# Average pooling, 2x2x2: three 16-row, 512 B stores on ScalarE's queue in place of one 2 KB-a-row store

One core of one Trainium2 chip. The metric is device time in microseconds of the whole program, lower is better; the kernel before takes 91.7 us.

## The reference

`x` is (8, 32, 32, 32, 32) float32, 33.55 MB; the kernel size is 2. Each output element is the mean of a 2x2x2 window, so the output is (8, 32, 16, 16, 16), 4.19 MB.

```python
for i in range(out_d):
    for j in range(out_h):
        for k in range(out_w):
            window = x[:, :, 2*i:2*i+2, 2*j:2*j+2, 2*k:2*k+2]
            result[:, :, i, j, k] = np.mean(window, axis=(-3, -2, -1))
```

## The kernel before

The 256 (batch, channel) rows are two halves `t` of 128 partitions. Each half is read in four units of 32 KB a row; the last two units are each read as two half loads of 16 KB. Five input buffers are in turn. VectorE pools each unit into `obuf[t]` (16 KB a row) with three instructions. All loads go through SyncE's queue. One store of 2 KB a row goes through ScalarE's queue as soon as the fifth unit is pooled; the others follow the loads on SyncE's queue.

```python
plan = [
    (0, 0, (32,)), (0, 32, (32,)), (0, 64, (32,)), (0, 96, (32,)),
    (1, 0, (32,)), (1, 32, (32,)), (1, 64, (16, 16)), (1, 96, (16, 16)),
]
# pool_unit: tensor_add over d, tensor_add over w, tensor_tensor_reduce over h with scale 0.125
for t, k0, parts in plan:
    tin = pool_in.tile([P, 32 * KF], F32, tag="tin", name="tin")
    # one nc.sync.dma_start for each part, then pool_unit for each part   (cut)
for queue, t, k0, kb in [
    (nc.scalar, 1, 0, 2),
    (nc.sync, 0, 0, 16),
    (nc.sync, 1, 2, 12),
    (nc.sync, 1, 14, 2),
]:
    queue.dma_start(
        out=ov[t * P:(t + 1) * P, k0 * KF:(k0 + kb) * KF],
        in_=obuf[t][:, k0 * KF:(k0 + kb) * KF],
    )
```

`KF` is 256 elements, 1 KB. A scheduler places every issue where its data is ready; each store waits for its units.

Of the kernel before, what the change touches and what calls it, by code (L numbers as in the profile page):

```python
# [1 line left out]

# [4 lines left out]

F32 = mybir.dt.float32
KF = 256


@with_exitstack
def pool_rows(
    ctx: ExitStack,
    tc: tile.TileContext,
    x: bass.AP,
    kernel_size: int,
    out: bass.AP,
):
    nc = tc.nc  # L20
    assert kernel_size == 2, "only kernel_size == 2 supported"

    B, C, D, H, W = x.shape
    P = nc.NUM_PARTITIONS
    assert (B * C, D, H, W) == (2 * P, 32, 32, 32)
    add = mybir.AluOpType.add



    xv = x.rearrange("b c d h w -> (b c) (d h w)")  # L30
    ov = out.rearrange("b c d h w -> (b c) (d h w)")




    pool_in = ctx.enter_context(tc.tile_pool(name="pin", bufs=5))
    pool_out = ctx.enter_context(tc.tile_pool(name="pout", bufs=1))
    obuf = [pool_out.tile([P, 16 * KF], F32, name=f"obuf{t}") for t in range(2)]
    dummy = pool_out.tile([P, 1], F32, name="dummy")


    plan = [
        (0, 0, (32,)),
        (0, 32, (32,)),
        (0, 64, (32,)),
        (0, 96, (32,)),
        (1, 0, (32,)),
        (1, 32, (32,)),
        (1, 64, (16, 16)),
        (1, 96, (16, 16)),  # L50
    ]

    def pool_unit(buf, t, k0, kb):

        od = kb // 8
        a = buf.rearrange("p (o dd e) -> p o dd e", o=od, dd=2)
        b = buf[:, :od * 1024]
        nc.vector.tensor_add(  # L58
            out=b.rearrange("p (o e) -> p o e", o=od), in0=a[:, :, 0], in1=a[:, :, 1])
        bv = b.rearrange("p (e ww) -> p e ww", ww=2)  # L60
        c = buf[:, od * 1024:od * 1536]
        nc.vector.tensor_add(out=c, in0=bv[:, :, 0], in1=bv[:, :, 1])  # L62
        cv = c.rearrange("p (j hh k) -> p j hh k", hh=2, k=16)
        o0 = k0 * KF // 8
        nc.vector.tensor_tensor_reduce(  # L65
            out=obuf[t][:, o0:o0 + od * 256].rearrange("p (j k) -> p j k", k=16),
            in0=cv[:, :, 0], in1=cv[:, :, 1],
            scale=0.125, scalar=0.0, op0=add, op1=add, accum_out=dummy[:, :],
        )

    for t, k0, parts in plan:
        tin = pool_in.tile([P, 32 * KF], F32, tag="tin", name="tin")
        views = []
        o = 0
        for kb in parts:
            v = tin[:, o * KF:(o + kb) * KF]
            nc.sync.dma_start(  # L77
                out=v, in_=xv[t * P:(t + 1) * P, (k0 + o) * KF:(k0 + o + kb) * KF])
            views.append((v, k0 + o, kb))
            o += kb  # L80
        for v, k, kb in views:
            pool_unit(v, t, k, kb)



    for queue, t, k0, kb in [
        (nc.scalar, 1, 0, 2),
        (nc.sync, 0, 0, 16),
        (nc.sync, 1, 2, 12),
        (nc.sync, 1, 14, 2),  # L90
    ]:
        queue.dma_start(
            out=ov[t * P:(t + 1) * P, k0 * KF:(k0 + kb) * KF],
            in_=obuf[t][:, k0 * KF:(k0 + kb) * KF],
        )


def kernel(tc: tile.TileContext, x: bass.AP, kernel_size: int, out: bass.AP):
    nc = tc.nc
    pool_rows(tc, x, kernel_size, out)  # L100
    tc.close()
    tc.compile()  # L102
    blocks = nc.main_func.blocks



    opening, program = blocks[0].instructions, blocks[tc.starting_block_idx].instructions
    load = next(i for i in program if isinstance(i, mybir.InstDMACopy))
    assert load.engine == nc.sync.engine
    barrier = next(  # L110
        n for n, i in enumerate(opening)
        if i.engine == load.engine and isinstance(i, mybir.InstDrain))
    program.remove(load)
    opening.insert(barrier, load)




    closing = blocks[-1].instructions
    stores = [  # L120
        i for i in program
        if isinstance(i, mybir.InstDMACopy) and "out_" in i.outs[0].memref]
    kept = [u.id for i in stores for u in i.sync_info.on_update]
    kept = [n for j, n in enumerate(kept) if n not in kept[j + 1:]]
    final = next(
        i for i in closing
        if i.engine == nc.sync.engine and isinstance(i, mybir.InstDrain))
    waits = {w.id: w for w in final.sync_info.on_wait}
    closing[closing.index(final)] = mybir.InstDrain(
        name=final.name, engine=final.engine, ins=[], outs=[], is_reset_sema=False,  # L130
        sync_info=mybir.SyncInfo(
            on_wait=[w for n, w in waits.items() if n not in kept], on_update=[]))


    reset = next(
        n for n, i in enumerate(closing)
        if isinstance(i, mybir.InstDrain) and i.is_reset_sema)
    first, stop = closing[reset].reset_range_start, closing[reset].reset_range_stop
    assert isinstance(closing[reset + 1], mybir.InstISA)
    while len(closing) > reset:  # L140
        closing.pop()
    n = first
    while n < stop:
        m = n
        while m < stop and m not in kept:
            m += 1
        if m > n:
            closing.append(mybir.InstDrain(
                name=nc.get_next_instruction_name(), engine=nc.gpsimd.engine, ins=[], outs=[],
                is_reset_sema=True, reset_range_start=n, reset_range_stop=m))  # L150
            nc.gpsimd.sem_clear(range(n, m))
        n = m + 1
    for n in kept:
        w = waits[n]
        closing.append(mybir.InstEventSemaphore(
            name=nc.get_next_instruction_name(), engine=nc.sync.engine, ins=[], outs=[],
            sync_info=mybir.SyncInfo(
                on_wait=[w],
                on_update=[mybir.SyncUpdate(
                    sync_type="semaphore", id=n, ant_name=w.ant_name,  # L160
                    update_mode="sem-sub-imm", update_value=w.wait_value)])))


# [1 line left out]
_INS = ['x', 'kernel_size']  # L165
_OUTS = [((8, 32, 16, 16, 16), 'float32')]

_NUMBERS = {'kernel_size': 2}


# [26 lines left out]
```

## Time and profile before

| | before |
|---|---|
| time, median of 6 runs | 91.68 us (91.52 to 91.82) |
| VectorE busy | 64.1 us (74%) |
| DMA, SyncE's queue / ScalarE's queue | 98.4% / 0.8% of sixteen engines |
| HBM read / written | 33.55 / 4.19 MB |

The page's DMA shares are shares of the time of all sixteen DMA engines. The span of the profile (86.6 us) ends before the last store lands, at 90.4; a landing is the time of issue plus the page's "us to landing". The lines themselves stand in the prediction.

### The profile page before, as it was taken

How to read it: one execution, taken by the hardware profiler on the slowest of the kernel's cores; microseconds unless marked ns; L12 is line 12 of the kernel's file. 1: busy time of each engine (PE TensorE's matmuls, PEld its weight loads, DVE VectorE, ACT ScalarE, POOL GpSimd, SP SyncE). 2: the span in 40 equal slices, each digit the busy share in tenths (PEclk: the TensorE clock that was granted, in tenths of full speed). 3: DMA queues.
4: the chain of work that ended last, by engine and by line, in shares of the span. 5: the costliest groups of instructions: out<-in, count | busy, mean ns of one | idle time of the engine just before them, and what ended most of it. 6: DMA issues, size and time to landing. Idle time of an engine off the chain costs nothing.

```text
span 86.6 us, 91 instructions
## 1 busy us (share of the span) xinstructions
DVE 64.1 (74%) x40; POOL 0.2 (0%) x4
## 2 busy tenths in 40 slices
DVE  0000049993999749992999749992999999999994
POOL 0000000000000000000000000000000000000000
DMA  8889998899979999799988999699999999999999
GB/s 242 379 363 469 485 485 348 379 485 485 469 333 409 485 485 424 318 469 485 485 348 379 485 485 469 288 454 416 405 407 424 407 462 394 462 394 454 394 454 398
DMA packets 1774, 36.48 MB, mean 421 GB/s; under 512 B 192, under 2 KB 192, under 8 KB 320
## 3 DMA queue, kind: packets, MB, share of 16 engines
q1 hardware_dynamic: 1630, 36.22, 98.4%
q10 hardware_dynamic: 144, 0.26, 0.8%
HBM read 33.55 MB, written 4.19 MB: 436 GB/s over the span
## 4 chain that ended last, share of the span: by engine, by line
DMA 83%; DVE 14%; SPq 1%; issue 0%; DVEq 0%
DMA tin<-in_x_dram 83%; DVE tin L58 8%; DVE tin L62 4%; DVE obuf L65 2%; SPq L77 1%; DVE dummy L65 0%; DVEq L102 0%
## 5 line engine op out<-in xcount | busy, mean ns | idle before, releaser
L58 DVE TENSOR_TENSOR tin<-tin 128x4096 f32<-128x4096 f32 (+1 forms) x10 | 35.7, 3570 | 20.7 <-DMA tin<-in_x_dram 20.6
L62 DVE TENSOR_TENSOR tin<-tin 128x2048 f32<-128x2048 f32 (+1 forms) x10 | 18.6, 1865 | 0.3
L65 DVE CUSTOM_DVE_ANT_1 obuf<-tin 128x1024 f32<-128x1024 f32 (+1 forms) x10 | 10.1, 1011 | 0.3
L65 DVE DVE_READ_ACCUMULATOR2_ANT dummy<- 128x1 f32 x10 | 0.8, 82 | 0.0
L178 POOL MEMSET const-uint8-127<- 128x1 uint8 x1 | 0.1, 102 | 0.0
L178 POOL MEMSET const-bfloat16-1.0<- 128x1 bf16 x1 | 0.1, 101 | 0.0
L178 POOL MEMSET const-float32-0.0<- 128x1 f32 x1 | 0.1, 98 | 0.2 <-issue 0.2
L178 POOL MEMSET const-float32-1.0<- 128x1 f32 x1 | 0.1, 98 | 0.0
## 6 DMA issues: line engine op xcount, KB each, us to landing
tin<-in_x_dram SPq DMA_DIRECT2D x6, 4096.0 KB, 35.0
tin<-in_x_dram SPq DMA_DIRECT2D x4, 2048.0 KB, 38.9
out_dram<-obuf SPq DMA_DIRECT2D x1, 2048.0 KB, 36.8
out_dram<-obuf SPq DMA_DIRECT2D x1, 1536.0 KB, 8.8
out_dram<-obuf ACTq DMA_DIRECT2D x1, 256.0 KB, 9.9
out_dram<-obuf SPq DMA_DIRECT2D x1, 256.0 KB, 4.9
```

The costliest lines, as they stand in the source:

```text
L58: nc.vector.tensor_add(out=b.rearrange("p (o e) -> p o e", o=od), in0=a[:, :, 0], in1=a[:, :, 1])
L62: nc.vector.tensor_add(out=c, in0=bv[:, :, 0], in1=bv[:, :, 1])
L65: nc.vector.tensor_tensor_reduce(out=obuf[t][:, o0:o0 + od * 256].rearrange("p (j k) -> p j k", k=16), in0=cv[:, :, 0], in1=cv[:, :, 1], s ...
L77: nc.sync.dma_start(out=v, in_=xv[t * P:(t + 1) * P, (k0 + o) * KF:(k0 + o + kb) * KF])
L178: nc = _bacc.Bacc("TRN2", target_bir_lowering=False, num_devices=1)
```

## The change

Its intent is to let only tiny transfers come between the loads, and to keep the 256 KB for the tail. Three stores of 16 rows x 512 B go out on ScalarE's queue after the first, third and fifth unit; the full SyncE stores write the same bytes once more later.

```diff
-    for queue, t, k0, kb in [
-        (nc.scalar, 1, 0, 2),
-        (nc.sync, 0, 0, 16),
-        (nc.sync, 1, 2, 12),
-        (nc.sync, 1, 14, 2),
-    ]:
-        queue.dma_start(
+    for t, k0 in [(0, 0), (0, 8), (1, 0)]:
+        nc.scalar.dma_start(
+            out=ov[t * P:t * P + 16, k0 * KF:k0 * KF + 128],
+            in_=obuf[t][:16, k0 * KF:k0 * KF + 128])
+    for t, k0, kb in [(0, 0, 16), (1, 0, 14), (1, 14, 2)]:
+        nc.sync.dma_start(
             out=ov[t * P:(t + 1) * P, k0 * KF:(k0 + kb) * KF],
             in_=obuf[t][:, k0 * KF:(k0 + kb) * KF],
         )
```

## The prediction

> **What bounds the kernel now.** I began with the page's summary, because it says which resource is full. VectorE is busy 74% of the span, the DMA row is at 8 or 9 tenths nearly everywhere, and the scalar queue (q10) is a very small part of the traffic:
>
> ```profile
> DVE 64.1 (74%) x40; POOL 0.2 (0%) x4
> DMA packets 1774, 36.48 MB, mean 421 GB/s; under 512 B 192, under 2 KB 192, under 8 KB 320
> q1 hardware_dynamic: 1630, 36.22, 98.4%
> q10 hardware_dynamic: 144, 0.26, 0.8%
> ```
>
> 98.4% and 0.8% make 99.2% of sixteen engines' time over the whole span. To see whether that is a plateau or an average, I took the timeline, where each 4 MB load releases one large addition on VectorE:
>
> ```profile
> 12.12 4.42 DVE L58 TENSOR_TENSOR tin<-tin 128x4096 f32<-128x4096 f32 x1 [12.12 <-DMA tin<-in_x_dram]
> 21.81 4.43 DVE L58 TENSOR_TENSOR tin<-tin 128x4096 f32<-128x4096 f32 x1 [1.68 <-DMA tin<-in_x_dram]
> 31.53 4.43 DVE L58 TENSOR_TENSOR tin<-tin 128x4096 f32<-128x4096 f32 x1 [1.70 <-DMA tin<-in_x_dram]
> ...
> 60.67 4.43 DVE L58 TENSOR_TENSOR tin<-tin 128x4096 f32<-128x4096 f32 x1 [1.69 <-DMA tin<-in_x_dram]
> ...
> 80.95 0.08 DVE L65 DVE_READ_ACCUMULATOR2_ANT dummy<- 128x1 f32 x1
> ...
> 81.18 2.29 DVE L58 TENSOR_TENSOR tin<-tin 128x2048 f32<-128x2048 f32 x1
> ```
>
> The loads land 9.71 us apart (21.81 less 12.12, and so on; five intervals take 48.55 us), and VectorE idles 1.7 us in each. One load is 4.194 MB, so the rate is 432 GB/s. The busy share by windows agrees and places the one irregular stretch:
>
> ```profile
> 31.53:41.25 9.72, 7.95 (x5) 0.00 (x0) 1.00 1.00 432
> 50.96:60.67 9.71, 7.95 (x5) 0.00 (x0) 1.00 0.98 420
> 60.67:81.18 20.51, 20.16 (x17) 0.00 (x0) 1.00 1.01 425
> 81.18:86.60 5.42, 4.21 (x4) 0.00 (x0) 1.00 0.95 406
> ```
>
> (Columns: stretch, length, VectorE busy, GpSimd busy, clock, DMA share, GB/s.) The share is 1.00 wherever there are only loads.
>
> The chain of waits ends in VectorE's last 4.3 us, which suggests a tail of "last load, pool, store". That is misleading, and the list of DMA issues shows why:
>
> ```profile
> out_dram<-obuf SPq DMA_DIRECT2D x1, 2048.0 KB, 36.8
> out_dram<-obuf SPq DMA_DIRECT2D x1, 1536.0 KB, 8.8
> out_dram<-obuf ACTq DMA_DIRECT2D x1, 256.0 KB, 9.9
> out_dram<-obuf SPq DMA_DIRECT2D x1, 256.0 KB, 4.9
> ```
>
> The timeline has SyncE issuing these three stores at 49.3, 81.1 and 85.5 us. They land at 49.3 + 36.8 = 86.1, 81.1 + 8.8 = 89.9 and 85.5 + 4.9 = 90.4. The 2 MB store sits behind the loads in SyncE's queue and lands 86.1 - 81.18 = 4.9 us after the last load, which is 2.097 MB at 432 GB/s; the 1.5 MB store takes the next 3.8 us, and the 256 KB the last 0.5. So the engines go from loads to stores without a pause, and the last store was in the queue some 4 us before they got to it. The end is set by the sum of bytes through sixteen full engines: 37.75 MB / 432 GB/s = 87.4 us. The rest of 91.57 is the start (12.12 less one period, 2.4 us), some small costs and 1.2 us after the last landing.
>
> **What the Trainium skill says.** "DMA: Bandwidth & Descriptors", section "Where 436 GB/s comes from", gives 435.2 GB/s as the ceiling of sixteen SBUF ports; the measured 432 is 99% of it, so the loads have nothing left to gain. The same page, "Issuing engines are not separate DMA queues", says that transfers issued on ScalarE and SyncE run on the same sixteen engines and interleave. The trace agrees: the ScalarE store, issued at 59.0 amid loads, took 9.9 us to land for bytes that need 0.6. Its section "Queues, rings and completion order" says each engine goes round its queues packet by packet; so a tiny store costs its own packet and cannot hold up the loads for long. "Specifications" puts the size for line rate at 512 B and above, just what each tiny row has; no run yet shows one here.
>
> **The change part by part.** All per engine, since the engines share each transfer equally; a 16-row store gives each engine one row if it is spread over all sixteen.
>
> 1. *Removed: the 256 KB store on ScalarE.* q10 took 0.8% of 86.6 us = 0.69 us of each engine. It had 144 / 16 = 9 packets per engine, and the bytes alone need 0.262 MB / 432 GB/s = 0.61 us, so a packet costs about 0.009 us beyond its bytes. Minus 0.69.
> 2. *Moved: those 256 KB into the second SyncE store*, 12 KB a row becoming 14 KB, with no packets added. Plus 0.61. Items 1 and 2 give -0.08.
> 3. *The interruption of the loads.* From 60.67 to the last load's release at 81.18 are 20.51 us. The two units of two half loads each are two periods, 19.42; the ScalarE store is 0.69; the half-size packets double the data packets from 16 to 32 per engine, 16 x 0.009 = 0.14. That leaves 0.26 us unaccounted for. It is in the stretch where the ScalarE store entered (DMA share 0.98 and 420 GB/s just before 60.67). If the store caused it, removing it is worth up to -0.26; if the smaller load packets did, 0.
> 4. *Added: three tiny stores.* 512 B at 27 GB/s per engine is 0.019 us, plus a data and a semaphore packet at 0.009 each: 0.037, three times 0.11. If an interruption costs by the event, up to 3 x 0.26 = 0.78 more; by the packet (one against eight), 3 x 0.03 = 0.10.
> 5. *Waits.* The three tiny stores take part in the rotation of completion semaphores. The instruction order of the changed kernel shows that a later half load then also waits for the first tiny store, the last half load for the fourth load, the 2 MB store for the second tiny one and the next store for the third. The last half load's issue, now at about 40, is put off to the landing at 41.25. Nothing comes of it: it lands 41 us after issue, four transfers deep. The tiny stores come from units done at about 20, 40 and 59, and are waited for at about 30, 49 and 81; even with the 9.9 us that the old store took they are in time.
> 6. *VectorE* runs the same 42 instructions; 64.1 us with slack. The last load may land 0.7 to 0.9 us earlier since the 256 KB are now behind it, but that only lengthens the last store's time in the queue.
>
> The sum with item 3 at half and item 4 by the packet: -0.08 - 0.13 + 0.11 + 0.10 = 0.00. Tiny stores among full-size loads are less likely to disturb than nine packets in a row of half loads, so I lean to a small gain: 91.5 us.
>
> **The rivals.**
> - *A shorter tail.* One could say that loads released 0.8 us earlier make the end 0.8 us earlier: 90.8. For it speaks the chain of waits, which passes through the last load and VectorE. Against it the landing times: the stores pour out at full rate until 90.4 with their issues some 4 us early, and the 256 KB that left the loads' way are in that tail.
> - *Every entry of the second queue costs by the event.* Then three cost up to 0.78 and the removal gives 0.26 back: about 92.0. For it speaks only the 0.26 of item 3, which is not shown to be the store's.
> - *A tiny store is late and holds a load or a store back.* Something must then be late by more than the queue's depth, two whole loads (about 19 us) at the half loads' issue; a stall would show as DMA below 1.00 and cost microseconds, 94 or more. Against it stand the margins of item 5, 9 us or more each.
> - *The early writes spare a later cost*, of the first write to each stretch of output. In the kernel before, the 2 MB store writes a part of the output never written before and still lands at the full-rate 4.9 us, so nothing is there to spare; it would be 91.5 again.
>
> **Range and chances.** The terms are tenths of a microsecond and their signs partly cancel; the three runs before span 0.3 us. I put 91.5, from 91.1 to 92.0. Two per cent is 1.8 us, more than twice the largest term in either direction, and I know nothing in the profile that could give it except a stall from the waits. Faster 0.02, same 0.96, slower 0.02.
>
> **What would show it right or wrong.** Right: loads still 9.71 us apart; q10 at about 0.1% instead of 0.8%; the larger store's landing about 0.6 us later after the 2 MB store's than now, and the last landing within 0.3 us of 90.4; the last load's release near 80.4. Item 3 is decided by the stretch from the sixth load's release to the last half load's: 19.6 if the store caused the excess, 19.8 if not. Wrong: a dip of the DMA share at an issue of SyncE, load periods longer than 9.8 after a tiny store, or an end that moves by more than 0.5 us with the same DMA share.

## The result, and the profile after

| | before | after |
|---|---|---|
| time, median of 6 runs | 91.68 us (91.52 to 91.82) | 92.10 us (92.05 to 92.27) |
| ratio | | 1.0051, 95% interval 1.0037 to 1.0065 |

A ratio is the mean time of one kernel's runs over that of the other's runs of the same rounds, so it is not quite the ratio of the medians. Executions over 1.5% slower than the fastest of the same kernel are left out of the means. The change costs 0.4 us: within 2%, as expected, but 0.1 us above the predicted range, and in the direction that I had not leaned to.

DMA queues and issues in the page of the changed kernel:

```profile
q1 hardware_dynamic: 1633, 36.35, 99.2%
q10 hardware_dynamic: 96, 0.02, 0.1%
...
out_dram<-obuf SPq DMA_DIRECT2D x1, 2048.0 KB, 36.5
out_dram<-obuf SPq DMA_DIRECT2D x1, 1792.0 KB, 9.0
out_dram<-obuf SPq DMA_DIRECT2D x1, 256.0 KB, 5.4
out_dram<-obuf ACTq DMA_DIRECT2D x3, 8.0 KB, 6.4
```

ScalarE's share fell to 0.1% as foreseen, and the engines are as full as they were. The SyncE stores were issued at 49.3, 81.1 and 85.3 us, so they land at 85.8, 90.1 and 90.7. Before it was 86.1, 89.9 and 90.4. The 2 MB store is 0.3 us earlier, not the 0.7 to 0.9 by which the prediction let the last load land earlier, and the larger second store then turns that into 0.3 us later.

Where the missing 0.5 us went is seen in windows of 4 us: the one in which the ScalarE store entered (60 to 64) and the one just ahead of the first big SyncE store (76 to 80). The last two columns are the DMA share and GB/s. Before:

```profile
60.00:64.00 4.00, 3.33 (x1) 0.00 (x0) 1.00 0.97 381
...
76.00:80.00 4.00, 3.93 (x5) 0.00 (x0) 1.00 1.07 451
```

After:

```profile
60.00:64.00 4.00, 3.30 (x1) 0.00 (x0) 1.00 0.99 420
64.00:76.00 12.00, 11.90 (x10) 0.00 (x0) 1.00 1.02 433
76.00:80.00 4.00, 3.93 (x5) 0.00 (x0) 1.00 0.97 356
```

A packet counts in the window in which it starts, so neither column alone is safe in a short window; GB/s over the share is. It is the rate of the sixteen engines while they are busy: 433 / 1.02 = 425 among half loads, and 381 / 0.97 = 393 and 356 / 0.97 = 367 in the two bad windows. So the engines are not idle there, but their load packets take longer. In 76 to 80 us of the changed kernel the loss is 4 x 0.97 x (1 - 367/425) = 0.53 us of every engine; in the kernel before it is nothing there (451 / 1.07 = 421) and 4 x 0.97 x (1 - 393/425) = 0.29 us at 60 to 64.

The packets in the trace say it exactly (in the kernel before and after, a packet is one row's piece of a transfer on one engine, or a semaphore's update, the signal that an engine has done its share). A 16 KB load packet takes 0.611 us nearly everywhere, but two in a row on most engines (one on the others) took 0.8 to 1.1 us; they started from 77.5 to 79 us, just before the last load's shares landed (80.15 to 80.95 us). I call the sum of such excess, over all packets and divided by sixteen engines, the *stretch*: 0.58 us in 74 to 82 us after the change, against 0.07 there and 0.34 at 58 to 74 before it. The engines also part company: the last half load's sixteen shares land within 0.80 us of each other (before 0.39), the last store's within 0.77 (before 0.42). The program ends 1.39 us after the *slowest* engine's last landing in both, so what counts is 90.37 against 90.70. The mean of the last store's sixteen landings moved less, from 90.11 to 90.25: the other 0.19 us of the 0.33 come from engines that lost unequally (in the second profiles of both kernels, shown further down, the mean moves by 0.09 of 0.13 us).

### The profile page after: what moved, and what is told of

Its sections match the earlier page's. It is cut to its first block, busy times and chain, and to the rows that moved or that the text cites. A ratio compares the mean times of both kernels' runs of the same rounds, so it can differ in the third digit from the quotient of the medians.

```text
span 86.4 us, 94 instructions
## 1 busy us (share of the span) xinstructions
DVE 64.0 (74%) x40; POOL 0.2 (0%) x4
## 4 chain that ended last, share of the span: by engine, by line
DMA 61%; DVE 37%; issue 0%; DVEq 0%
DMA tin<-in_x_dram 61%; DVE tin L58 21%; DVE tin L62 11%; DVE obuf L65 6%; DVE dummy L65 0%; DVEq L102 0%
```

## The experiments

My theory after this (A): when the loads first meet a bulk store, every engine loses some half microsecond, once. The old ScalarE store took that loss early and more cheaply; the tiny stores do not. Its rival (C): the tiny stores, their semaphores (the counters by which an engine waits for a transfer) or the later issue of the last half load are to blame. Four kernels at a time shared a chip and the runs of the kernel before. The edits below are abridged and show what differs from the changed kernel. Each kernel has one profile, of one execution.

**No tiny stores** (e1_none).

```diff
-    for t, k0 in [(0, 0), (0, 8), (1, 0)]:
-        nc.scalar.dma_start(...)
```

> The changed kernel without its three tiny stores; the 2 KB are still in the second SyncE store. Theory A (the 256 KB store on ScalarE paid early for a cost that comes when loads first meet a store over all 128 rows; the tiny stores do not pay it, so it is paid by the last half load now): 92.0 us, the tiny stores' 0.11 us gone and nothing else; DMA in 76 to 80 us as in the changed kernel (356 GB/s at a share of 0.97). Theory C (the tiny stores themselves, their semaphore order or the later issue of the last half load slow it): 91.5 us, and 450 GB/s in 76 to 80 us.

Measured: 91.97 us (91.87 to 92.15), ratio to before 1.0028 (1.0015 to 1.0041).

```profile
76.00:80.00 4.00, 3.93 (x5) 0.00 (x0) 1.00 0.97 352
```

The slow window is there with no tiny store in the program. C falls for the larger part: about 0.26 us of the slowdown is there without them. The rest is 0.08 to 0.13 us by the medians of the changed kernel (92.05 and 92.10) and 0.07 to 0.21 by the ratios, which agrees with the 0.11 of the prediction but is not measured more closely than that.

**One ScalarE store of 128 rows x 512 B** (e2_128rows_512B).

```diff
+    nc.scalar.dma_start(out=ov[P:2 * P, 0:128], in_=obuf[1][:, 0:128])   # for the tiny ones
```

> One store on ScalarE of 128 rows of 512 B from the fifth unit in place of the three tiny ones, eight packets per engine, written again by the full SyncE store. Theory A (rows or packets per engine count): the cost is paid near 60 us, 76 to 80 us goes at about 450 GB/s, and the time is 91.9 us (0.11 off, 0.23 on for the packets, 0.34 off for the cost). Theory B (it is the bytes that count, and 64 KB are too few): 76 to 80 us stays near 356 GB/s and the time is 92.2 us.

Measured: 92.13 us, ratio 1.0042 (1.0027 to 1.0057), 356 GB/s at 0.97 in 76 to 80 us. In this profile eight packets of 512 B per engine, on all rows, did not take the loss early.

**One ScalarE store of 16 rows x 16 KB** (e3_16rows_16KB).

```diff
+    nc.scalar.dma_start(out=ov[0:16, 0:4096], in_=obuf[0][:16, 0:4096])   # for the tiny ones
```

> One store on ScalarE of 16 rows of 16 KB from the first half's finished output (ready at 49 us), as many bytes as the old 2 KB store but one packet per engine; written again by SyncE, so 0.62 us of engine time more. Theory B (bytes count): 76 to 80 us at about 450 GB/s, 92.3 us. Theory A (rows or packets count): 76 to 80 us at about 356 GB/s, 92.6 us.

Measured: 92.61 us (92.26 to 92.68, five runs), ratio 1.0084 (1.0066 to 1.0102); a sixth run, at 93.83, is not used.

```profile
48.00:52.00 4.00, 2.21 (x3) 0.00 (x0) 1.00 1.09 410
...
76.00:80.00 4.00, 3.93 (x5) 0.00 (x0) 1.00 0.97 418
```

In this profile a single 16 KB packet per engine goes with a loss at another place: the rate while busy is 376 GB/s at 48 to 52 us, and 431 where the changed kernel had 367. In the trace the stretch is 0.50 us at 50 to 52 us and 0.005 in 74 to 82. So here the loss is taken once, and nothing of it returns after the 24 us of loads that follow. My reading, "by the first store that is big enough", is not shown: the next kernels speak against it. The time of 92.6 shows that taking it early earns nothing by itself: it lies 0.64 us above the kernel without tiny stores, and the extra packets are 0.62. One thing more differs: SyncE's 2 MB store waited for this store and was issued at 57.2 us and not at 49.3, still some 24 us before the engines came to it.

**The 2 KB store, from the first unit at 20 us** (e4_early_2KB).

```diff
+    nc.scalar.dma_start(out=ov[0:P, 0:512], in_=obuf[0][:, 0:512])        # for the tiny ones
+    # SyncE: (0, 512:4096), (1, 0:3584), (1, 3584:4096)
```

> The 2 KB store on ScalarE as in the kernel before, but from the first unit at 20 us (output rows of the first half) and not from the fifth at 59 us; nothing is written twice. If an early store over all rows pays the cost for good (theory A): 91.7 us, like the kernel before, with 76 to 80 us at about 450 GB/s. If it must lie close before the big stores, or on the other half's rows: 92.0 us with 76 to 80 us near 356 GB/s.

Measured: 92.04 us, ratio 1.0027 (1.0014 to 1.0040), 365 GB/s at 0.98 in 76 to 80 us; stretch 0.09 us at 24 to 32 us and 0.52 in 74 to 82. The same number of bytes at another time, and for the other half of the rows, neither takes the loss nor helps. My theory A in its simple form, "any early bulk store over all rows", falls.

**The 2 KB store at 49 us** (g1_2KB_at49).

```diff
+    nc.scalar.dma_start(out=ov[0:P, 3584:4096], in_=obuf[0][:, 3584:4096])
+    # SyncE: (0, 0:3584), (1, 0:3584), (1, 3584:4096)
```

> The 2 KB store on ScalarE taken from the fourth unit at 49 us instead of the first at 20; nothing written twice. If an early bulk store helps only when it comes close before the big stores (theory T, time): it pays near 53 us or later, 76 to 80 us goes at about 450 GB/s, 91.7 us. If what counts is that it meets 16 KB load packets and not 32 KB ones (theory L): its packets mostly meet 32 KB loads (from 53 to 60 us), 76 to 80 us stays at or near 356 GB/s, 92.0 us.

Measured: 91.99 us, ratio 1.0018 (1.0001 to 1.0036), 401 GB/s at 1.02 in 76 to 80 us, stretch 0.23 us up to 58 us and 0.33 in 74 to 82. The loss is split in two here, in an execution that took 91.72 us, the fastest of the six; the median is the time that theory L gave, the window lies between.

**16 rows x 4 KB** (g2_16rows_4KB).

```diff
+    nc.scalar.dma_start(out=ov[0:16, 0:1024], in_=obuf[0][:16, 0:1024])   # for the tiny ones
```

> As the 16 rows of 16 KB, with 4 KB a row: one 4 KB packet per engine at 49 us, written again by SyncE (0.16 us of engine time). If the cost is an amount that is paid in parts (theory S): about 0.15 us of longer load packets near 50 us, 0.4 us left for 76 to 80 us (some 380 GB/s), 92.1 us. If it is paid in one go by whatever is big enough (theory E): either nothing near 50 us and 356 GB/s in 76 to 80 us, 92.1 us, or all of it near 50 us and 420 GB/s or more in 76 to 80 us, 92.1 us as well; the windows decide, not the time.

Measured: 92.06 us, ratio 1.0026 (1.0009 to 1.0042), 389 GB/s at 1.00 in 76 to 80 us. I had overlooked that 4 KB a row is all from the first unit, so this store went out at 20 us and not at 49. Its own packets left no mark (0.01 us of stretch at 22 to 24), and stretches of 0.43 us in all from 38 to 64 us had no store packet near them. They did not spare the loss of 0.39 in 74 to 82 us. It decides nothing between S and E, and it speaks against theory A: load packets are also lengthened where no store enters.

**1 KB a row at 59 us** (g3_1KB_at59).

```diff
+    nc.scalar.dma_start(out=ov[P:2 * P, 0:256], in_=obuf[1][:, 0:256])
+    # SyncE: (0, 0:4096), (1, 256:3584), (1, 3584:4096)
```

> The kernel before with 1 KB a row instead of 2 KB in the ScalarE store at 59 us, the rest in the second SyncE store; nothing written twice. Theory S: half of the 0.3 us near 60 us and 76 to 80 us between 356 and 451 GB/s, near 400; 91.85 us. Theory E: like the kernel before or like the one without tiny stores, 91.7 or 92.0 us.

Measured: 91.95 us (91.54 to 92.26), ratio 1.0009 (0.9984 to 1.0034), in its profile (at 92.15) 369 GB/s at 1.05 and a stretch of 0.77 us in 74 to 82. Executions of one kernel differ by 0.7 us here. That the loss varies as much from one to the next is likely, but not shown, as one of them was profiled. Nothing of it was taken early in this profile, against S.

**The early 2 KB store, third and fourth load split** (g4_early_2KB_halfloads).

```diff
-        (0, 64, (32,)),  (0, 96, (32,)),
+        (0, 64, (16, 16)),  (0, 96, (16, 16)),     # and the store as in e4_early_2KB
```

> The early 2 KB store from the first unit at 20 us, with the third and fourth loads split into two halves each, so that its packets meet 16 KB load packets. Splitting adds 16 packets per engine (0.14 us). Theory L (16 KB load packets): about 0.3 us of longer load packets near 24 us, 76 to 80 us at about 450 GB/s, 91.85 us. Theory T (time): 356 GB/s in 76 to 80 us, 92.2 us.

Measured: 91.82 us (91.73 to 92.22), ratio 1.0013 (0.9994 to 1.0032): the time of theory L. Its windows were not: 393 GB/s at 1.01 in 76 to 80 us, with a stretch of 0.37 in 74 to 82 and 0.10 before 58.

**The 2 KB store put back beside two tiny ones** (h1_tiny_and_2KB), the most direct test.

```diff
-    for t, k0 in [(0, 0), (0, 8), (1, 0)]:     # the third tiny store becomes
+    for t, k0 in [(0, 0), (0, 8)]:             # 128 rows x 2 KB again
+    nc.scalar.dma_start(out=ov[P:2 * P, 0:512], in_=obuf[1][:, 0:512])
+    # SyncE: (0, 0:4096), (1, 512:3584), (1, 3584:4096)
```

> The changed kernel with its third tiny store widened back to the 256 KB store (128 rows of 2 KB, which then leaves the second SyncE store); the first two tiny stores, the rotation of semaphores and the later issue of the last half load stay. Theory A (the loss is the missing 2 KB store): 91.75 us, the kernel before plus two tiny stores of 0.037; 76 to 80 us at about 450 GB/s. Theory C (the tiny stores or their waits): 92.0 us or more.

Measured: 91.85 us (91.72 to 91.86), ratio 1.0008 (0.9995 to 1.0022).

```profile
60.00:64.00 4.00, 3.29 (x1) 0.00 (x0) 1.00 1.03 430
76.00:80.00 4.00, 3.93 (x5) 0.00 (x0) 1.00 1.02 393
```

On the same chip the changed kernel took 92.05 (91.97 to 92.22) and the kernel before 91.84 and 91.74. With the same rotation of semaphores and the same late half load as the changed kernel, the time is that of the kernel before. What slows the changed kernel is the missing 2 KB store; why it does, this does not show. The window of 450 GB/s that I expected did not come: that store makes the loss smaller, and does not always take it early.

**Two 2 KB stores, at 49 and 59 us** (h2_two_2KB).

```diff
+    # ScalarE: (0, 3584:4096) and (1, 0:512), 128 rows each
+    # SyncE: (0, 0:3584), (1, 512:3584), (1, 3584:4096)
```

> Two 2 KB stores on ScalarE over all 128 rows, from the fourth unit at 49 us and from the fifth at 59, nothing written twice. If each takes a share of the switch's cost and lets the engines arrive at it closer together: 91.5 to 91.7 us, and 76 to 80 us at 450 GB/s. If an early store merely moves the cost: 91.7 to 91.8 us.

Measured: 91.79 us, ratio 1.0003 (0.9989 to 1.0018), 426 GB/s at 1.05. No gain over one, which answers the question of a better version: none was found.

**Both kernels once more** (h3_before_again, h4_after_again; no edit).

> The kernel before once more, for a second profile. If its smooth passage into the big stores is a property and not one lucky profile: 91.7 us, 76 to 80 us at 440 GB/s or more, last landings of the sixteen engines within 0.45 us of each other. If not: anything from 356 to 451 GB/s.

> The changed kernel once more, for a second profile. If the slow switch is a property: 92.1 us, 76 to 80 us at about 356 GB/s, last landings spread over 0.6 us or more. If it is chance: as the kernel before in some profiles.

Measured: before 91.84 us, ratio 1.0008 (0.9993 to 1.0023); after 92.05 us, ratio 1.0036 (1.0022 to 1.0051). The windows of the second profile of before, then of after:

```profile
60.00:64.00 4.00, 3.36 (x1) 0.00 (x0) 1.00 1.03 432
76.00:80.00 4.00, 3.93 (x5) 0.00 (x0) 1.00 1.00 393
```

```profile
60.00:64.00 4.00, 3.03 (x1) 0.00 (x0) 1.00 0.99 420
76.00:80.00 4.00, 3.93 (x5) 0.00 (x0) 1.00 1.00 381
```

The difference in time repeats. The smooth passage of the first profile of before was luck: in this one the loss sits in front of the big stores as well, only smaller (stretch 0.34 in 74 to 82 us, against 0.47 after; last landings within 0.55 and 0.59 us). One profile of each kernel had shown me a cleaner story than there is.

**Control: no ScalarE store, third and fourth load split** (i2_none_halfloads).

```diff
-        (0, 64, (32,)),  (0, 96, (32,)),
+        (0, 64, (16, 16)),  (0, 96, (16, 16)),     # and no store on ScalarE
```

> Control: no store on ScalarE at all, third and fourth loads split in halves (0.16 us of packets more than the kernel without tiny stores, 91.97). If the split loads alone gave the relief: 91.8 us. If it takes the 2 KB store meeting half loads (theory L): 92.1 us.

Measured: 91.88 us (91.74 to 91.99), ratio 1.0009 (0.9992 to 1.0025), stretch 0.35 us in 74 to 82. That is 0.08 us over the kernel before by the ratio, where the unsplit kernel without early stores was at 0.26 and has 0.16 us less of packets: splitting two loads of the middle helps without any early store. Theory L is not needed to explain the time of the split kernel with the early store (91.82), and falls.

**The 2 KB store at 49 us, fifth and sixth load split** (i1_2KB_at49_halfloads).

```diff
-        (1, 0, (32,)),  (1, 32, (32,)),
+        (1, 0, (16, 16)),  (1, 32, (16, 16)),      # and the store as in g1_2KB_at49
```

> The 2 KB store from the fourth unit at 49 us, with the fifth and sixth loads split in halves so that its packets meet 16 KB load packets. Theory L: 91.9 us (0.16 for the split, 0.3 off against the 92.1 that the unsplit one would give). Otherwise 92.1 us or more.

Measured: 91.85 us (91.55 to 92.12), ratio 1.0008 (0.9988 to 1.0028); stretch 0.49 us up to 58 us, 0.004 in 74 to 82. The time fits L, but after the control it cannot speak for it.

**The first big store begun with 2 KB a row** (i4_small_first).

```diff
+    # no store on ScalarE; SyncE: (0, 0:512), (0, 512:4096), (1, 0:3584), (1, 3584:4096)
```

> No store on ScalarE; the first big SyncE store is cut into 2 KB of each row, then 14 KB, so the switch begins with 2 KB packets (0.07 us more). If the loss comes from the large first store packet: 91.75 us and 76 to 80 us above 400 GB/s. If not: 92.05 us.

Measured: 91.93 us (91.68 to 92.36), ratio 1.0017 (0.9994 to 1.0040). Inconclusive; the profile (of a run at 91.68) has 360 GB/s at 0.92 in 76 to 80 us, a stretch of 0.31.

**The 2 KB store at 59 us, written again in the tail** (i5_2KB_twice).

```diff
+    nc.scalar.dma_start(out=ov[P:2 * P, 0:512], in_=obuf[1][:, 0:512])    # SyncE as in the changed kernel
```

> The 2 KB store on ScalarE at 59 us as before, but the second SyncE store writes those bytes again, so the tail stays as long as in the changed kernel and only the store's presence differs (0.68 us of packets). If presence counts: 92.3 us. If it is the 256 KB taken out of the tail: 92.65 us.

Measured: 92.33 us (92.29 to 92.53), ratio 1.0063 (1.0049 to 1.0078).

```profile
60.00:64.00 4.00, 3.37 (x1) 0.00 (x0) 1.00 0.97 377
76.00:80.00 4.00, 3.93 (x5) 0.00 (x0) 1.00 1.03 442
```

It is the presence of the store that counts, not the 256 KB that it takes out of the tail. The time is 0.36 us above the kernel without early stores, where its packets alone would cost 0.68. Here the loss was taken early, at 60 to 64 us (389 GB/s while busy), and none of it later (429).

**All together.** The *engine work* is the sum of every packet at its usual time (32 KB 1.213 us, 16 KB 0.611, 14 KB 0.535, 12 KB 0.460, 2 KB 0.084, 512 B 0.027, a semaphore's 0.009), divided by sixteen. The *remainder* is the median time less that: start, end and whatever the engines lost.

| kernel | median us | engine work | remainder | stretch at 3-58 / 58-74 / 74-82 us |
|---|---|---|---|---|
| before | 91.68 | 87.81 | 3.87 | 0.07 / 0.34 / 0.07 |
| before, second | 91.84 | 87.81 | 4.03 | 0.05 / 0.08 / 0.34 |
| 2 KB beside two tiny (h1) | 91.85 | 87.89 | 3.96 | 0.01 / 0.10 / 0.41 |
| two 2 KB (h2) | 91.79 | 87.89 | 3.90 | 0.13 / 0.13 / 0.22 |
| 2 KB twice (i5) | 92.33 | 88.41 | 3.92 | 0.12 / 0.42 / 0.00 |
| 2 KB at 20, split (g4) | 91.82 | 87.97 | 3.85 | 0.10 / 0.10 / 0.37 |
| 2 KB at 49, split (i1) | 91.85 | 87.97 | 3.88 | 0.49 / 0.00 / 0.00 |
| none, split (i2) | 91.88 | 87.90 | 3.98 | 0.12 / 0.09 / 0.35 |
| after | 92.10 | 87.84 | 4.26 | 0.02 / 0.07 / 0.58 |
| after, second | 92.05 | 87.84 | 4.21 | 0.03 / 0.06 / 0.47 |
| none (e1) | 91.97 | 87.73 | 4.24 | 0.06 / 0.08 / 0.62 |
| 128 rows x 512 B (e2) | 92.13 | 87.96 | 4.17 | 0.05 / 0.04 / 0.57 |
| 16 rows x 16 KB (e3) | 92.61 | 88.35 | 4.26 | 0.77 / 0.00 / 0.01 |
| 2 KB at 20 (e4) | 92.04 | 87.81 | 4.23 | 0.11 / 0.03 / 0.52 |
| 2 KB at 49 (g1) | 91.99 | 87.81 | 4.18 | 0.23 / 0.01 / 0.33 |
| 16 rows x 4 KB (g2) | 92.06 | 87.90 | 4.16 | 0.36 / 0.12 / 0.39 |
| 1 KB at 59 (g3) | 91.95 | 87.81 | 4.14 | 0.04 / 0.05 / 0.77 |
| 2 KB first in the tail (i4) | 91.93 | 87.81 | 4.12 | 0.04 / 0.09 / 0.31 |

The table is sorted by the remainder: 3.85 to 4.03 us in the upper eight rows, 4.12 to 4.26 in the lower ten. The gap of 0.09 us is less than the 0.16 between the two medians of the one kernel before, so the line between them is not sharp. A second count uses the ratios, which compare runs of the same rounds: the time over the kernel before, less the engine work over it. It is within 0.1 us of zero in the upper rows. It is 0.23 to 0.44 us, clear of zero by the 95% intervals, for the changed kernel twice, e1, e2, e3 and e4. It is 0.17 for g1, just clear, and 0.08 to 0.16 for g2, g3 and i4, which are undecided. All four kernels that have the 2 KB store at 59 us are in the upper rows.

The stretch is of one profiled run and the median of all runs, so they match only roughly; and it is a mean over engines, while the time follows the slowest. In all eighteen profiles the program ended 1.37 to 1.40 us after the slowest engine's last landing.

## Why the prediction was wrong

- **The bound and the sum of bytes: right.** The engines are full from the first load to the last store. The end after the last landing is 1.39 us, not 1.2: the prediction took the landing from the profiled run (91.76 us) and the time from a median of 91.57. The packets of items 1, 2 and 4 come to 87.84 - 87.81 = +0.03 us of engine work, where the prediction had -0.69 + 0.61 + 0.11 = +0.03.
- **Item 3 and the fourth rival: the step that failed.** Item 3 saw 0.26 us unaccounted for where the ScalarE store entered, and called its removal worth "up to -0.26; if the smaller load packets did, 0". It has the opposite sign: without any ScalarE store (e1) the time is 0.26 us above the kernel before, although its packets are 0.08 us less. For the changed kernel the remainder rose by 0.2 to 0.4 us (3.87 to 4.26; in the repeats, 4.03 to 4.21), and putting the 2 KB store back brought it down to 3.96. The window that item 3 leaned on, 420 GB/s at 0.98 just before 60.67 us, was no sign of the store: its first packet started at 62.64, and the kernel with no ScalarE store has 422 at 0.98 in the same window (50.93 to 60.64). The fourth rival had the right kind of effect, an early write that spares a later cost (its reason, the first write to each stretch of output, is not shown; e4 writes early as well and spares nothing). I dismissed it with "nothing is there to spare", because the 2 MB store lands 4.9 us after the last load, at full rate. That looked on the wrong side of the switch: the engines lose their time in the last loads, before the first store packet, and a landing difference that begins at the last load cannot show it. The loss in the kernel before had also been there, at 60 to 64 us in the first profile, and I read it as the price of the interruption; in the second profile the stretch at 58 to 74 us is 0.08 and not 0.34, so it is no fixed price of that store.
- **Item 4, tiny stores: right.** They leave no stretch of their own (0.02 us in 3 to 58 us, where two of them enter), and cost about the 0.11 us of their packets: 92.10 and 92.05 with them, 91.97 without. The 0.78 us of an interruption that costs by the event are excluded. Each of their 512 B packets took 0.027 us, 19 GB/s on its engine, against 26.8 for a 16 KB packet; so the size that the prediction took from the Trainium skill ("DMA: Bandwidth & Descriptors", "Specifications") as enough for line rate does not reach it here, though the prediction's sum, with 0.009 us a packet, had this right (0.028).
- **Items 5 and 6, waits and VectorE: right.** Loads up to the sixth land at the old pace (9.73 us at most), the first two tiny stores are in by 26.6 and 46.1 us for waits at 30 and 49, and the last half load, issued at 41.25, was never short of work ahead of it. VectorE is as busy as before (64.0 us).
- **The signs that I named.** ScalarE's queue at 0.1%: yes. The larger store 0.6 us further behind the 2 MB store: 4.3 against 3.8 us, yes. The last landing within 0.3 us of 90.4: 90.70, at the very edge. The last load near 80.4, 0.7 to 0.9 us earlier: no, 80.95 on the slowest engine, 0.2 us earlier. From the sixth load to the last half load 19.6 or 19.8 us: no, 20.3, and this is the step at which the prediction came apart.
- **The range.** It carried the sum of small terms but no term for a loss at the switch. The scatter of the runs does not excuse the miss: of eleven runs of the changed kernel (91.97 to 92.27 us) one is below 92.0.

What stays open: why the 2 KB store at 59 us, or split loads in the middle, make the loss at the switch smaller, and what sets its size in one execution. Row count, bytes, time of the store and size of the load packets that it meets were each tried, and none alone sorts the kernels; the time of the store was never changed without also changing which half of the output it writes. That the loss is taken once fits the profiles in which it moved (e3, i5, i1) and not those in which it came in two places (g1, g2). In the first profile of before, in i5 and in e3 most of the lengthened load packets start before the ScalarE store's first packet, by up to 2 to 4 us (60.5 to 62.9 us against 62.64, 59.6 to 62.9 against 62.61, 49.3 to 52.0 against 53.27), as those of the changed kernel do ahead of the 2 MB store; what in the DMA engines that is, no run here shows.

## What to carry to other kernels

Where the DMA engines are full from end to end, read a transfer's worth from the packets of every engine and not from the chain of waits, and look at the slowest engine's last landing. When a store among the loads seems to cost something, ask whether that is its own price or a price that some later store will pay instead; compare GB/s over the busy share on both sides of the place where loads give way to stores. And below 0.5% take a second profile of both kernels before building a theory on one.

## What the Trainium skill lacked or had wrong

- "DMA: Bandwidth & Descriptors" has nothing on a loss where a stream of loads gives way to bulk stores. Here load packets were lengthened by 0.4 to 0.9 us for each engine, summed over an execution from 3 us on, most of it near such places, though all sixteen engines were busy throughout; a 16 KB packet went from 0.611 to as much as 1.09 us in the changed kernel.
- Same page, "Latency and other measured facts", gives about 600 ns to the first byte for transfers issued by SyncE and ScalarE. Here the first load's first packet came 1.0 us after the start of the instruction that issues it, which is 0.63 us after its end, so the trace agrees if one counts from the end; the page does not say from where. The first tiny store's, issued amid loads, came 3.5 us after the start (20.16 to 23.64), and it landed 6.4 us after it. The page has no figure for a transfer issued while the engines are full.
- No page says that the engines, which share each transfer equally, can drift apart at such a switch: in the changed kernel the sixteen shares of the last load but one landed within 0.44 us of each other and those of the last within 0.80. It is not so in every execution: in its second profile both are 0.69.
